# Four expert pairs of a mixture layer sent to their tokens through DRAM instead of by products, in a two-layer decoder trunk on one Trainium2 core

## The chip, the cores and the metric

The kernel runs on one core of a Trainium2 chip. The metric is device time in microseconds (us) of one execution: the median of the kernel before is 1228.84 us over three runs (1222.7 to 1231.54). Engines are named as in the profile: PE (TensorE products), PEld (its weight loads), DVE (VectorE), ACT (ScalarE), POOL (GpSimd), SP (SyncE, which here only issues transfers).

## The reference, cut to what matters

Two layers run on 512 tokens of width 1024. Each has a mixer (attention and gated linear attention) and then a mixture of 32 SwiGLU experts, of which each token uses two. What the change touches is the mixture:

```python
comb = (one_hot(grp_idx, N_GROUPS)[:, :, None] * exp_w[:, None, :])      # two nonzero weights a token
y = zeros_like(hf)
for g in range(N_GROUPS):                                                # 4 groups of 8 experts
    a = einsum('nd,edf->nef', hf, w_gate[g])
    u = einsum('nd,edf->nef', hf, w_up[g])
    y = y + einsum('nef,efd->nd', silu(a) * u * comb[:, g, :, None], w_down[g])
x = x + gate_f * y
```

An expert's weights are three matrices of 1 MB (1024 x 256 in float32): gate, up and down. A layer reads 96 of them.

## The kernel before, in words

The mixture of one layer is `moe`. Tokens are first routed. Each expert has 64 slots, two experts make a pair (128 slots, one per partition), and 16 pairs are worked off in order 0 to 15. I call the position in that order a place. The normalised tokens lie in DRAM (`xg`). For each place:

- `fetch` (POOL, an indirect transfer) brings the rows of the 128 slots, four at first and then two every second place. `gather` turns them with eight PE transposes (tile `g`) and writes them with scale and shift as `gT` (DVE and ACT by turns).
- `hidden`, L1012 on: 16 written products (tile `gu`, 32 instructions in the trace) against gate and up of the two experts; then `silu` on ACT and a product on DVE give `hs`.
- `turn`: two transposes (tile `hsT`) and an ACT copy give `hT`.
- `down`: 8 written products (tile `d`, 16 in the trace) against the down matrices. DVE multiplies by the slots' weights and the gate (L1063, tile `o`); ACT and POOL split that into two float32r halves (L1068 `ohi`, L1069 `olo`).
- `places` builds on DVE a 128x512 matrix with a one where a slot belongs to a token (L1086, L1088), and `combine` multiplies it with the halves: 16 products (tile `y`) for the 8 pieces of 128 tokens x 512 columns, each added to the tokens' rows by DVE (L1076, `add`).

The order on PE is written out. In the loop's step i stand: `down` of place i-1, `hidden` of place i, then the eight `combine` pieces of place i-1 with the transposes of the next gather and `turn` of place i between them. The matmuls made by `pm` keep that order.

The weights come by one queue, SP, in the order of the list `queue`, one 1 MB transfer per matrix. Gate and up share a buffer of 16 KB a partition (`wgu`, five buffers, so two and a half pairs); down has four (`wd`, two pairs). A transfer of `wgu` waits until `hidden` has read the buffer five experts before; one of `wd` until `down` has read the buffer four experts before. SP issues in order: what waits holds up all behind it. The first nine loads are queued ahead of the routing, later ones four at a time after each `hidden`.

```python
queue = [(0, 0), (0, 1), (0, 2), (0, 3), (0, 4), (1, 0), (1, 1), (1, 2), (1, 3)]
for i in range(0, NE, 2):
    queue += [(0, e) for e in (i + 5, i + 6) if e < NE] + [(1, e) for e in (i + 4, i + 5) if e < NE]
```

The tuple's first number is 0 for gate and up, 1 for down; the second is the expert. The last place's products are joined with those of the place before in `combine_last`. Sums and rows of tokens stay in SBUF (`xt`); float32 throughout.

Of the kernel before, what the change touches and what calls it, by code (L numbers as in the profile page):

```python
# [20 lines left out]
P = 128  # L21
# [4 lines left out]
NX = 16  # L26


@with_exitstack
def hybrid_decoder_kernel(ctx, tc, x, c, w_ada, b_ada, norm_mix, norm_ffn, w_in, w_gk2, b_gk, q_gain,  # L30
# [182 lines left out]
    xg = dram.tile([S, D], F, name="xg")  # L213

# [648 lines left out]
    def moe(l, xt, ss, pool):  # L863
# [11 lines left out]
        for i in range(0, NE, 2):  # L875
            queue += [(0, e) for e in (i + 5, i + 6) if e < NE] + [(1, e) for e in (i + 4, i + 5) if e < NE]
# [13 lines left out]
        def load_weights(n):  # L890
            for _ in range(min(n, len(queue))):
                w, e = queue.pop(0)
                loaded[w, e] = load_expert(w, lambda src: src[l, e // 8, e % 8])
# [149 lines left out]
        def down(hT, ws, i=None):  # L1043
# [7 lines left out]
            for q in range(2):  # L1051
# [5 lines left out]
                o = ot([P, 512], name="o")  # L1057
# [4 lines left out]
                else:  # L1062
                    V.scalar_tensor_tensor(o, pd, cws[:, i:i + 1], gate, op0=OP.mult, op1=OP.mult)  # L1063
# [19 lines left out]
        def places(i):  # L1083

            o1 = s2([P, S], name="o1")
            V.tensor_scalar(o1, slots_row[:, 0], sid[:, i:i + 1], None, op0=OP.is_equal)  # L1086
            oT = (rows_ if i == NE // 2 - 1 else ohs)([P, S], R, name="oT")
            V.scalar_tensor_tensor(oT, slots_row[:, 1], sid[:, i:i + 1], o1, op0=OP.is_equal, op1=OP.add)  # L1088
            return oT
# [11 lines left out]
        def combine_last(pairs):  # L1101
# [18 lines left out]
            for n, u in ((0, 5), (0, 6), (1, 0), (1, 1), (0, 7), (1, 2), (1, 3), (1, 4), (1, 5), (1, 6), (1, 7)):  # L1120
                unit(n, u)

# [79 lines left out]
        fetched = [fetch(idx[:, i:i + 1]) for i in range(4)]  # L1202


        with tc.issue_after(listed.ins), tc.issue_after(normed.ins):
# [16 lines left out]
            dump(f"cw{l}", cw)  # L1222
            exw = tmp.rearrange("p t k e -> p (t k) e")
# [22 lines left out]
        hs = None  # L1246
        for i in range(NE // 2):
            while not {(0, 2 * i), (0, 2 * i + 1)} <= set(loaded):
                load_weights(1)
            if i % 2 == 0:  # L1250
                now = gT
                if i < NE // 2 - 2:
                    gT, rest = gather(fetched[i + 2:i + 4])
                    fetched += [fetch(idx[:, j:j + 1]) for j in range(i + 4, min(i + 6, NE // 2))]

            if i:
                part = places(i - 1), down(hT, [loaded.pop((1, e)) for e in (2 * i - 2, 2 * i - 1)], i - 1)
            *_, hs = hidden(gT1 if i == 1 else now, 0 if i < 2 else P * (i % 2), [loaded.pop((0, e)) for e in (2 * i, 2 * i + 1)])
            load_weights(4)
# [5 lines left out]
            if i == 0:  # L1265
                for _ in second:
                    pass
                weights_by_slot()
            for u in range(4):
                for v in range(2):  # L1270
                    if i:
                        combine(2 * u + v, *part)
                next(rest, None)
                if u == 2:
                    hT = turn(hs)
        last = []
# [95 lines left out]
```

## Time and profile before

| what | value |
|---|---|
| median of three runs | 1228.84 us (1222.7 to 1231.54) |
| the profiled execution | 1228.59 us |
| its span, first to last instruction | 1226.4 us |
| mean granted TensorE clock | 0.988 of full |
| PE busy | 1174.6 us, 96% of the span |
| DVE, ACT, POOL busy | 56%, 39%, 16% |
| weights of both mixtures | 2 x 96 transfers of 1 MB, all issued by SP |

Times in the rows are us from the span's start. Layer 1's mixture runs products from about 374 to 625 us, layer 2's from about 968 to the end. "DMA share" in a stretch is the mean busy share of the core's 16 DMA engines, and GB/s what they moved. A releaser in brackets is what ended an idle time. One `issue to landing` is the time of a transfer from its issue to its semaphore.

### The profile page before, as it was taken

To read this page: it belongs to the slowest core of one execution; us is meant where nothing else is said; L and a number is where in the kernel's file an instruction comes from. 1 tells how busy PE (TensorE), PEld (TensorE's weight loads), DVE (VectorE), ACT (ScalarE), POOL (GpSimd) and SP (SyncE) were. 2 spreads that over 40 slices of the span, in tenths; PEclk is the share of its full clock that TensorE was granted. 3 is DMA by queue.
4 is the path that set the end of the run, shared out by engine and by line. 5 is a ranking of instruction groups with operands and counts; after the bars stand their busy time and mean duration, and the time that the engine had idled before them with its cause. 6 is when DMAs were issued, how large, how long until landed. Compare 5 with 4: busy or idle time off the path is not lost.

```text
span 1226.4 us, 17270 instructions
## 1 busy us (share of the span) xinstructions
PE 1174.6 (96%) x6467; PEld 749.3 (61%) x6467; DVE 686.3 (56%) x1336; ACT 473.6 (39%) x942; POOL 196.7 (16%) x231
## 2 busy tenths in 40 slices
PE   4999999999989999999999997999999899999997
PEld 3787867666765444444478775666876744444443
DVE  3474546465854555555566562545856565555553
ACT  4376656453243111111155764554624411111121
POOL 3000010011312222221110001001210222222110
PEclk8999999999999999999999999999999999999999
DMA  9652765643687999999445355563229599999981
GB/s 297 225 170 88 223 167 148 207 142 101 249 369 263 411 410 417 419 418 419 191 156 173 98 168 121 172 172 121 69 103 372 210 400 420 418 420 419 419 349 69
DMA packets 105926, 312.27 MB, mean 255 GB/s; under 512 B 12876, under 2 KB 49936, under 8 KB 81264
## 3 DMA queue, kind: packets, MB, share of 16 engines
q1 hardware_dynamic: 96720, 289.57, 63.4%
q0 software_dynamic: 9120, 21.57, 5.2%
q8 instruction: 52, 0.85, 0.3%
q14 instruction: 34, 0.28, 0.1%
HBM read 311.08 MB, written 8.40 MB: 260 GB/s over the span
## 4 chain that ended last, share of the span: by engine, by line
PE 85%; DMA 6%; DVE 5%; ACT 2%; issue 1%; SPq 1%; DVEq 0%; ACTq 0%
PE proj L74 19%; PE gu L78 18%; PE y L78 10%; PE d L78 9%; PE op L74 6%; PE z L74 5%; DMA wada<-in_w_ada_dram 3%; PE ada L78 3%; PE g L1003 2%; DMA raw<-in_w_in_dram 2%; PE warm L78 1%; PE pv L74 1%; PE lgT L74 1%; PE o L74 1%; PE adaT L78 1%
## 5 line engine op out<-in xcount | busy, mean ns | idle before, releaser
L78 PE MATMUL gu<-wgu,gT 128*64 128x512 f32 x1024 | 225.4, 592 | 0.1
L74 PE MATMUL proj<-whl,hh 128*128 128x512 f32 (+2 forms) x768 | 218.6, 368 | 0.1
L78 PEld LDWEIGHTS gu<-wgu,gT 128*64 128x64 f32 x1024 | 75.5, 137 | 143.7 <-issue 142.2
L74 PEld LDWEIGHTS proj<-whl,hh 128*128 128x128 f32 x768 | 133.5, 189 | 32.0 <-issue 10.0
L1076 DVE TENSOR_TENSOR x<-y,x 128x512 f32<-128x512 f32 x240 | 148.5, 683 | 0.9 <-PE y L78 0.9
L74 PE MATMUL proj<-whl,hl 128*128 128x512 f32 (+2 forms) x384 | 138.4, 362 | 0.0
L1031 DVE TENSOR_TENSOR hs<-hs,gu 128x256 f32<-128x256 f32 x32 | 13.5, 421 | 198.2 <-ACT hs L1030 198.2
L1069 POOL TENSOR_TENSOR olo<-o,ohi 128x512 fp32r<-128x512 f32 x60 | 76.9, 1283 | 263.5 <-ACT ohi L1068 263.3
L96 DVE TENSOR_TENSOR whl<-raw,whl 128x512 fp32r<-128x512 f32 (+2 forms) x128 | 72.7, 570 | 81.8 <-ACT whl L95 70.5
L78 PE MATMUL d<-wd,hT 128*64 128x512 f32 x512 | 116.9, 598 | 1.4 <-ACT hT L1040 1.4
L78 PE MATMUL y<-ohi,oT 128*128 128x512 f32 x240 | 104.5, 436 | 0.0
L95 ACT ACTIVATE whl<-raw 128x512 fp32r<-128x512 f32 (+2 forms) x128 | 66.6, 524 | 85.1 <-PE proj L74 66.9
L78 PE MATMUL y<-olo,oT 128*128 128x512 f32 x240 | 94.2, 393 | 0.0
L74 PEld LDWEIGHTS proj<-whl,hl 128*128 128x128 f32 x384 | 72.2, 188 | 14.3 <-issue 4.2
L1030 ACT ACTIVATE hs<-gu 128x256 f32<-128x256 f32 x32 | 12.3, 385 | 168.4 <-PE gu L78 168.4
L78 PEld LDWEIGHTS d<-wd,hT 128*64 128x64 f32 x512 | 33.9, 136 | 62.2 <-issue 48.1
L78 PEld LDWEIGHTS y<-ohi,oT 128*128 128x128 f32 x240 | 45.4, 189 | 31.8 <-issue 26.0
L1009 ACT ACTIVATE gT<-g,mod 128x256 f32<-128x256 f32 (+1 forms) x72 | 38.9, 544 | 61.6 <-DVE gT L1011 61.5
L1068 ACT ACTIVATE ohi<-o 128x512 fp32r<-128x512 f32 x60 | 37.8, 630 | 61.6 <-DVE o L1063 61.6
L1063 DVE SCALAR_TENSOR_TENSOR o<-d,cws,gate_f 128x512 f32<-128x512 f32 x64 | 47.8, 750 | 22.7 <-PE d L78 22.7
L736 POOL TENSOR_TENSOR raw<-raw,gate_m 128x1024 f32<-128x1024 f32 x16 | 40.2, 2520 | 122.6 <-DMA raw<-in_w_out_dram 68.2
L78 PE MATMUL ada<-wada,ct 128*32 128x512 f32 x320 | 49.1, 600 | 5.3 <-DMA wada<-in_w_ada_dram 5.3
(346 smaller groups left out, 1951.9 us busy)
## 6 DMA issues: line engine op xcount, KB each, us to landing
wgu<-in_w_gate_dram SPq DMA_DIRECT2D x64, 1024.0 KB, 9.5
wgu<-in_w_up_dram SPq DMA_DIRECT2D x64, 1024.0 KB, 11.7
wd<-in_w_down_dram SPq DMA_DIRECT2D x64, 1024.0 KB, 11.0
wada<-in_w_ada_dram SPq DMA_DIRECT2D x96, 512.0 KB, 5.1
raw<-in_w_in_dram SPq DMA_DIRECT2D x80, 256.0 KB, 4.4
raw<-in_w_out_dram SPq DMA_DIRECT2D x16, 512.0 KB, 4.1
raw<-in_w_in_dram SPq DMA_DIRECT2D x32, 128.0 KB, 4.2
xg<-xn POOLq DMA_DIRECT2D x8, 512.0 KB, 4.9
```

The costliest lines, as they stand in the source:

```text
L74: T.matmul(o, a, b, start=start, stop=stop, skip_group_check=True)
L78: tc.keep_in_program_order(T.matmul(o, a, b, start=start, stop=stop, skip_group_check=True))
L95: A.activation(hi, src, AF.Copy)
L96: eng.tensor_tensor(lo, src, hi.bitcast(F), op=OP.subtract)
L736: G.tensor_tensor(t, t, gates[l, 2][:, None, cols].to_broadcast([P, 2, 512]), op=OP.mult)
L1003: tc.keep_in_program_order(T.transpose(ps[:, at:at + P], r[:, P * k:P * k + P], ident))
L1009: A.activation(o, src, AF.Identity, scale=m, bias=b)
L1031: V.tensor_tensor(hs[r], hs[r], gu[r, 256:512], op=OP.mult)
L1063: V.scalar_tensor_tensor(o, pd, cws[:, i:i + 1], gate, op0=OP.mult, op1=OP.mult)
L1068: A.activation(hi, o, AF.Copy)
L1069: (G if last is None else V).tensor_tensor(lo, o, hi.bitcast(F), op=OP.subtract)
L1076: V.tensor_tensor(xc, ps, xc, op=OP.add)
```

## The change

Expert pairs 0 to 3 (the constant `NY`) no longer go to the tokens by products. `ORDER` puts them at places 1, 4, 7 and 10; the other pairs keep the old way. For such a place `down` writes `o` into a slot of the pool that held `ohi` and `olo`, and POOL issues two transfers of 256 KB to a DRAM tile `ys` (128 rows of 4 KB per pair). There is no split, no `places` and no `combine`. Its `down` stands behind the next place's `hidden` instead of before it, so the remaining PE work of that step is four calls of the gather and `turn`.

From place 12 on `take_back` fetches, for each of four token tiles and two choices, the 128 rows that the tokens' slots name (POOL, indirect, rows out of bounds skipped), and DVE adds them times a 0/1 mask to the tokens' rows (128x1024). There are eight of these in a layer: two in each of steps 12 to 14, two behind the loop.

The list of loads follows the order in which buffers come free: before such a place's `down` the gate and up of the next load come first.

```diff
--- before.py
+++ after.py
@@ -24,6 +24,9 @@
 SBW, GKW, GVW, RANK, NIN = 512, 256, 512, 16, 3088
 NE, FE, CAP = 32, 256, 64
 NX = 16
+
+NY = 4
+ORDER = [4, 0, 5, 6, 1, 7, 8, 2, 9, 10, 3, 11, 12, 13, 14, 15]
 
 
 @with_exitstack
@@ -211,6 +214,7 @@
 
     xs = dram.tile([S, D], F, name="xs")
     xg = dram.tile([S, D], F, name="xg")
+    ys = dram.tile([NY * P, D], F, name="ys")
 
     mod = [const.tile([P, 6, KT], F, name=f"mod{l}") for l in range(L)]
     gates, gms, rowt = {}, {}, {}
@@ -872,8 +876,12 @@
         s1 = slots(pool, "s1", 4, 1024)
 
         queue = [(0, 0), (0, 1), (0, 2), (0, 3), (0, 4), (1, 0), (1, 1), (1, 2), (1, 3)]
-        for i in range(0, NE, 2):
-            queue += [(0, e) for e in (i + 5, i + 6) if e < NE] + [(1, e) for e in (i + 4, i + 5) if e < NE]
+
+        freed = [(0, 0)]
+        for i in range(1, NE // 2):
+            freed += [(0, i), (1, i - 1)] if ORDER[i - 1] < NY else [(1, i - 1), (0, i)]
+        for w, i in freed:
+            queue += [(w, e) for e in ((2 * i + 4, 2 * i + 5) if w else (2 * i + 5, 2 * i + 6)) if e < NE]
         loaded = {}
 
         def load_expert(which, src):
@@ -890,7 +898,8 @@
         def load_weights(n):
             for _ in range(min(n, len(queue))):
                 w, e = queue.pop(0)
-                loaded[w, e] = load_expert(w, lambda src: src[l, e // 8, e % 8])
+                n = 2 * ORDER[e // 2] + e % 2
+                loaded[w, e] = load_expert(w, lambda src: src[l, n // 8, n % 8])
 
         load_weights(9)
         wr, lc, lg = route.pop(l)
@@ -1054,13 +1063,17 @@
                     for e in range(n):
                         pm(pd[64 * e:64 * e + 64], hT[:, j, 64 * e:64 * e + 64],
                            ws[e][:, D * j + 512 * q:D * j + 512 * q + 512], j == 0, j == 1)
-                o = ot([P, 512], name="o")
+                m = NY if i is None else ORDER[i]
+                o = (ohl if m < NY else ot)([P, 512], name="o")
                 gate = gates[l, 5][r, 512 * q:512 * q + 512]
                 if i is None:
                     V.tensor_tensor(o[r], pd[r], gate, op=OP.mult)
                     parts.append(o)
                 else:
-                    V.scalar_tensor_tensor(o, pd, cws[:, i:i + 1], gate, op0=OP.mult, op1=OP.mult)
+                    V.scalar_tensor_tensor(o, pd, cws[:, m:m + 1], gate, op0=OP.mult, op1=OP.mult)
+                    if m < NY:
+                        kept_dma(G, ys[P * m:P * m + P, 512 * q:512 * q + 512], o)
+                        continue
                     if last is not None:
                         hi, lo = last[:, q, 0], last[:, q, 1]
                     else:
@@ -1083,9 +1096,10 @@
         def places(i):
 
             o1 = s2([P, S], name="o1")
-            V.tensor_scalar(o1, slots_row[:, 0], sid[:, i:i + 1], None, op0=OP.is_equal)
+            n = ORDER[i]
+            V.tensor_scalar(o1, slots_row[:, 0], sid[:, n:n + 1], None, op0=OP.is_equal)
             oT = (rows_ if i == NE // 2 - 1 else ohs)([P, S], R, name="oT")
-            V.scalar_tensor_tensor(oT, slots_row[:, 1], sid[:, i:i + 1], o1, op0=OP.is_equal, op1=OP.add)
+            V.scalar_tensor_tensor(oT, slots_row[:, 1], sid[:, n:n + 1], o1, op0=OP.is_equal, op1=OP.add)
             return oT
 
         units = [(tt, q) for tt in range(NT) for q in range(2)]
@@ -1119,6 +1133,16 @@
             yield
             for n, u in ((0, 5), (0, 6), (1, 0), (1, 1), (0, 7), (1, 2), (1, 3), (1, 4), (1, 5), (1, 6), (1, 7)):
                 unit(n, u)
+
+        ysi, ysm = pool.tile([P, NT, 2], I32, name="ysi"), t3(2, "ysm")
+
+        def take_back(tt, k):
+
+            r = rows_([P, D], name="back")
+            G.indirect_dma_start(r, None, ys[:, :], bass.IndirectOffsetOnAxis(ap=ysi[:, tt, k:k + 1], axis=0),
+                                 bounds_check=NY * P - 1, oob_is_err=False)
+            xc = xt[tt // 2][:, tt % 2]
+            return lambda: V.scalar_tensor_tensor(xc, r, ysm[:, tt, k:k + 1], xc, op0=OP.mult, op1=OP.add)
 
         def spread(slot, slot0):
 
@@ -1199,7 +1223,7 @@
         idx = pool.tile([P, NE // 2], I32, name="idx")
         listed = numbered(by_slot(exn, "nv"), idx)
         keep_warm(lo.rearrange("p t e -> p (t e)"), 20)
-        fetched = [fetch(idx[:, i:i + 1]) for i in range(4)]
+        fetched = [fetch(idx[:, i:i + 1]) for i in ORDER[:4]]
 
 
         with tc.issue_after(listed.ins), tc.issue_after(normed.ins):
@@ -1220,6 +1244,8 @@
             V.tensor_tensor(e2, e2, den, op=OP.mult)
             V.tensor_tensor(cw[:, :, 1:2], e2, gw, op=OP.mult)
             dump(f"cw{l}", cw)
+            V.tensor_scalar(ysi, slot, 65535.0, None, op0=OP.min)
+            V.tensor_scalar(ysm, slot, float(NY * P), None, op0=OP.is_lt)
             exw = tmp.rearrange("p t k e -> p (t k) e")
             V.tensor_tensor(exw, ex.rearrange("p t k e -> p (t k) e"), cw.rearrange("p t k -> p (t k)")[:, :, None].to_broadcast([P, NT * 2, NE]), op=OP.mult)
         cws = pool.tile([P, NE // 2], F, name="cws")
@@ -1243,7 +1269,7 @@
         for _ in rest:
             pass
         gT1, second = gather(fetched[1:2])
-        hs = None
+        back, taken = [(tt, k) for tt in range(NT) for k in range(2)], []
         for i in range(NE // 2):
             while not {(0, 2 * i), (0, 2 * i + 1)} <= set(loaded):
                 load_weights(1)
@@ -1251,11 +1277,14 @@
                 now = gT
                 if i < NE // 2 - 2:
                     gT, rest = gather(fetched[i + 2:i + 4])
-                    fetched += [fetch(idx[:, j:j + 1]) for j in range(i + 4, min(i + 6, NE // 2))]
-
-            if i:
+                    fetched += [fetch(idx[:, j:j + 1]) for j in ORDER[i + 4:i + 6]]
+
+            by_dram = i > 0 and ORDER[i - 1] < NY
+            if i and not by_dram:
                 part = places(i - 1), down(hT, [loaded.pop((1, e)) for e in (2 * i - 2, 2 * i - 1)], i - 1)
             *_, hs = hidden(gT1 if i == 1 else now, 0 if i < 2 else P * (i % 2), [loaded.pop((0, e)) for e in (2 * i, 2 * i + 1)])
+            if by_dram:
+                down(hT, [loaded.pop((1, e)) for e in (2 * i - 2, 2 * i - 1)], i - 1)
             load_weights(4)
             if i == 1:
                 overflow_lists()
@@ -1266,13 +1295,26 @@
                 for _ in second:
                     pass
                 weights_by_slot()
+            if by_dram:
+                for _ in range(4):
+                    next(rest, None)
+                hT = turn(hs)
+                continue
             for u in range(4):
                 for v in range(2):
                     if i:
                         combine(2 * u + v, *part)
+                if i >= NE // 2 - 4 and u % 2 == 0:
+                    taken.append(take_back(*back.pop(0)))
+                    if len(taken) > 1:
+                        taken.pop(0)()
                 next(rest, None)
                 if u == 2:
                     hT = turn(hs)
+        for tt, k in back:
+            taken.append(take_back(tt, k))
+        for add_back in taken:
+            add_back()
         last = []
         end = combine_last([part, last])
         next(end)
```

First, PE at places 9 to 11. Before, the steps of two places meet like this (`g` are the transposes of a gather, `hsT` those of `turn`):

```order
L1003 MATMUL g<-ident,rows 128x128 x2
L1038 MATMUL hsT<-ident,hs 128x128 x2
L78 MATMUL y<-ohi,oT 128x512
L78 MATMUL y<-olo,oT 128x512
L78 MATMUL y<-ohi,oT 128x512
L78 MATMUL y<-olo,oT 128x512
L1003 MATMUL g<-ident,rows 128x128 x2
L78 MATMUL d<-wd,hT 64x512 x8
L78 MATMUL gu<-wgu,gT 64x512 x16
L78 MATMUL y<-ohi,oT 128x512
L78 MATMUL y<-olo,oT 128x512
```

Now, where place 10 (expert pair 3) ends, the rows from the last two products of place 9 on are these:

```order
L81 MATMUL y<-ohi,oT 128x512
L81 MATMUL y<-olo,oT 128x512
L1012 MATMUL g<-ident,rows 128x128 x2
L81 MATMUL gu<-wgu,gT 64x512 x16
L81 MATMUL d<-wd,hT 64x512 x8
L1012 MATMUL g<-ident,rows 128x128 x8
L1047 MATMUL hsT<-ident,hs 128x128 x2
L81 MATMUL d<-wd,hT 64x512 x8
L81 MATMUL gu<-wgu,gT 64x512 x16
L81 MATMUL y<-ohi,oT 128x512
L81 MATMUL y<-olo,oT 128x512
```

The `d` of place 10 has moved behind the `gu` of place 11, the `d` of place 11 follows after ten transposes only, and no `y` of place 10 stands between them.

Second, SP's loads from expert 25 on. The numbers are the buffers' tiles; before, `wgu_4849` to `wgu_4960` are gate and up of experts 25 to 28 in places 12 to 14, and `wd_4855`, `wd_4857` are the down matrices of place 12:

```order
L887 DMA wgu_4849<-in_w_gate_dram 128x2048
L887 DMA wgu_4849<-in_w_up_dram 128x2048
L887 DMA wgu_4852<-in_w_gate_dram 128x2048
L887 DMA wgu_4852<-in_w_up_dram 128x2048
L883 DMA wd_4855<-in_w_down_dram 128x2048
L883 DMA wd_4857<-in_w_down_dram 128x2048
L887 DMA wgu_4957<-in_w_gate_dram 128x2048
L887 DMA wgu_4957<-in_w_up_dram 128x2048
L887 DMA wgu_4960<-in_w_gate_dram 128x2048
L887 DMA wgu_4960<-in_w_up_dram 128x2048
```

Now gate and up of places 12 to 14 are `wgu_4728` to `wgu_4737`, the down matrices of place 12 are `wd_4828` and `wd_4830`, those of place 13 `wd_4832` and `wd_4834`:

```order
L895 DMA wgu_4728<-in_w_gate_dram 128x2048
L895 DMA wgu_4728<-in_w_up_dram 128x2048
L895 DMA wgu_4731<-in_w_gate_dram 128x2048
L895 DMA wgu_4731<-in_w_up_dram 128x2048
L895 DMA wgu_4734<-in_w_gate_dram 128x2048
L895 DMA wgu_4734<-in_w_up_dram 128x2048
L895 DMA wgu_4737<-in_w_gate_dram 128x2048
L895 DMA wgu_4737<-in_w_up_dram 128x2048
L891 DMA wd_4828<-in_w_down_dram 128x2048
L891 DMA wd_4830<-in_w_down_dram 128x2048
L891 DMA wd_4832<-in_w_down_dram 128x2048
L891 DMA wd_4834<-in_w_down_dram 128x2048
```

The down matrices of place 12 stood ahead of the gate and up of experts 27 and 28, and now stand behind them: four more 1 MB transfers are ahead of them. The same holds at places 3, 6 and 9.

Third, POOL at the end of a mixture. Before, the last fetches and the halves:

```order
L983 DMA rows<-xg,idx 128x1024 x2
L1069 TENSOR_TENSOR olo<-o,ohi 128x512 x4
L983 DMA rows<-xg,idx 128x1024 x2
L1069 TENSOR_TENSOR olo<-o,ohi 128x512 x4
L983 DMA rows<-xg,idx 128x1024 x2
L1069 TENSOR_TENSOR olo<-o,ohi 128x512 x12
L1281 TENSOR_LOAD xcnt
```

Now, from the last fetches on (`ys` are the writes to DRAM, `back` the rows that come back):

```order
L91 DMA ys<-o 128x512 x2
L1082 TENSOR_TENSOR olo<-o,ohi 128x512 x2
L992 DMA rows<-xg,idx 128x1024 x2
L1082 TENSOR_TENSOR olo<-o,ohi 128x512 x2
L91 DMA ys<-o 128x512 x2
L1142 DMA back<-ys,ysi 128x1024
L1082 TENSOR_TENSOR olo<-o,ohi 128x512
L1142 DMA back<-ys,ysi 128x1024
L1082 TENSOR_TENSOR olo<-o,ohi 128x512
L1142 DMA back<-ys,ysi 128x1024
L1082 TENSOR_TENSOR olo<-o,ohi 128x512 x2
L1142 DMA back<-ys,ysi 128x1024 x4
```

The first `back` stands between the last two `ys` writes and the halves of place 11, and the others among the halves of places 11 to 13.

## Rows read from the trace of the kernel before

**Rows 1.** The page: busy time of PE over the span, then the granted clock, the DMA engines' busy share and their GB/s in 40 equal slices of 30.7 us.

```profile
PE 1174.6 (96%) x6467; PEld 749.3 (61%) x6467; DVE 686.3 (56%) x1336; ACT 473.6 (39%) x942; POOL 196.7 (16%) x231
...
DMA  9652765643687999999445355563229599999981
GB/s 297 225 170 88 223 167 148 207 142 101 249 369 263 411 410 417 419 418 419 191 156 173 98 168 121 172 172 121 69 103 372 210 400 420 418 420 419 419 349 69
```

**Rows 2.** Windows of layer 1's mixture: us, busy time of each engine (and its instructions), granted clock, DMA share, GB/s. The first lies ahead of the first product of an expert, when nine loads were queued at once; the last lies behind the mixture and holds a write to DRAM.

```profile
330.00:345.00 15.00, 15.00 (x72) 12.20 (x71) 11.58 (x19) 7.70 (x18) 0.00 (x0) 1.00 1.01 422
390.00:450.00 60.00, 60.00 (x290) 28.72 (x288) 35.53 (x67) 11.64 (x23) 14.15 (x12) 1.00 1.00 410
450.00:510.00 60.00, 60.00 (x289) 28.50 (x286) 32.57 (x58) 11.79 (x24) 14.22 (x12) 1.00 1.01 418
510.00:560.00 50.00, 50.00 (x241) 23.34 (x241) 29.36 (x53) 10.14 (x20) 9.65 (x8) 1.00 1.01 419
...
630.00:645.00 15.00, 14.14 (x86) 12.13 (x87) 11.46 (x22) 9.89 (x16) 3.13 (x5) 1.00 0.99 346
```

**Rows 3.** What SP's queue waited for, 390 to 560 us: waiter, releaser, us in total, times, longest.

```profile
SPq L883 <- PE d L78: 72.6, 11, 7.1
SPq L887 <- PE gu L78: 64.7, 11, 6.0
```

**Rows 4.** PE's timeline at one place of layer 1: start, us, line and operation, count.

```profile
551.98 0.50 PE L78 MATMUL y<-ohi,oT 128*128 128x512 f32 x1
...
556.99 3.65 PE L78 MATMUL d<-wd,hT 128*64 128x512 f32 x16
560.48 2.74 PE L78 MATMUL gu<-wgu,gT 128*64 128x512 f32 x12
```

**Rows 5.** PE's timeline elsewhere: eight transposes of a gather by themselves, and a `turn` with its `d` right behind it, with the wait between.

```profile
373.21 1.09 PE L1003 MATMUL g<-ident,rows 128*128 128x128 f32 x8 [0.19 <-DMA rows<-xg,idx]
...
615.35 0.39 PE L1038 MATMUL hsT<-ident,hs 128*128 128x128 f32 x2
616.20 3.65 PE L78 MATMUL d<-wd,hT 128*64 128x512 f32 x16 [0.46 <-ACT hT L1040]
```

**Rows 6.** The second down matrix of place 12 in layer 1: its issue on SP, then its transfer (KB, us from issue to landing), then the products that read it.

```profile
545.63 0.38 SPq L883 DMA_DIRECT2D wd<-in_w_down_dram  x1
...
wd<-in_w_down_dram SPq DMA_DIRECT2D x1, 1024.0 KB, 12.9
...
572.45 3.65 PE L78 MATMUL d<-wd,hT 128*64 128x512 f32 x16
```

**Rows 7.** The same three for layer 2.

```profile
1139.36 1.02 SPq L883 DMA_DIRECT2D wd<-in_w_down_dram  x1
...
wd<-in_w_down_dram SPq DMA_DIRECT2D x1, 1024.0 KB, 13.5
...
1166.18 3.65 PE L78 MATMUL d<-wd,hT 128*64 128x512 f32 x16
```

**Rows 8.** Layer 1's last gate and up load (expert 31): the issue of its up matrix, that transfer, and the first products of place 15, which read it.

```profile
583.38 0.42 SPq L887 DMA_DIRECT2D wgu<-in_w_up_dram  x1
...
wgu<-in_w_up_dram SPq DMA_DIRECT2D x1, 1024.0 KB, 10.4
...
605.97 1.46 PE L78 MATMUL gu<-wgu,gT 128*64 128x512 f32 x6
```

**Rows 9.** The page's groups of instructions: busy us, mean ns of one, idle time before them and its releaser.

```profile
L1076 DVE TENSOR_TENSOR x<-y,x 128x512 f32<-128x512 f32 x240 | 148.5, 683 | 0.9 <-PE y L78 0.9
L1069 POOL TENSOR_TENSOR olo<-o,ohi 128x512 fp32r<-128x512 f32 x60 | 76.9, 1283 | 263.5 <-ACT ohi L1068 263.3
L1063 DVE SCALAR_TENSOR_TENSOR o<-d,cws,gate_f 128x512 f32<-128x512 f32 x64 | 47.8, 750 | 22.7 <-PE d L78 22.7
```

**Rows 10.** Transfers issued by POOL: count, KB each, median us from issue to landing.

```profile
xg<-xn POOLq DMA_DIRECT2D x8, 512.0 KB, 4.9
xs<-x POOLq DMA_DIRECT2D x2, 1024.0 KB, 10.7
rows<-xg,idx POOLq DMA_INDIRECT x32, 8.6
```

**Rows 11.** The granted clock around three idle times of PE in layer 2 (columns as in rows 2).

```profile
757.50:762.80 5.30, 1.42 (x11) 0.91 (x10) 0.00 (x0) 0.00 (x0) 1.50 (x3) 1.00 0.61 58
762.80:769.60 6.80, 4.35 (x12) 3.23 (x12) 4.43 (x7) 4.62 (x9) 2.13 (x4) 0.50 0.48 122
889.00:892.40 3.40, 1.30 (x10) 0.49 (x8) 3.29 (x6) 0.54 (x1) 1.08 (x1) 1.00 0.19 26
892.50:895.90 3.40, 3.40 (x18) 2.29 (x15) 1.43 (x4) 0.60 (x1) 1.29 (x1) 0.50 0.34 127
957.40:960.80 3.40, 3.40 (x26) 3.17 (x25) 2.73 (x10) 0.00 (x0) 0.00 (x0) 0.50 0.39 161
```

**Rows 12.** Those idle times, in PE's timeline, and one that no fall of the clock followed (at 630.76).

```profile
765.25 1.11 PE L500 MATMUL qT<-ident,two 128*128 128x128 f32 x4 [6.33 <-ACT w L553]
...
891.29 2.08 PE L74 MATMUL pv<-w,v 128*64 128x512 f32 x8 [2.10 <-DVE mixl L96]
...
957.32 0.18 PE L78 MATMUL rk<-both,after_b 128*128 128x32 bf16 x1 [2.16 <-DVE both L951]
...
630.76 1.49 PE L78 MATMUL warm<-ident 128*128 128x128 f32 x11 [2.04 <-DVE sm L100]
```

## The prediction

> **What bounds the kernel now.** I read the page's slices first. PE is busy for 96% of the span, and in the slices of the two mixtures the DMA engines show a 9 as well, at 410 to 420 GB/s [rows 1]. So in just the stage that is changed two resources look full, and the question is which of them has room.
>
> The windows of layer 1's mixture say it more sharply. From 390 to 560 us PE is busy 60.00 of 60, 60.00 of 60 and 50.00 of 50 us: it waits for no weight at all. The DMA share is 1.00 to 1.01, at 410 to 419 GB/s. When nine loads had been queued at once, ahead of the first expert product, with none waiting for a buffer, the rate was 422 GB/s [rows 2]. So 420 is what this core's DMA moves when it is never short of requests, and the mixture runs at it. SP does wait for PE to release buffers, 72.6 us for `d` and 64.7 us for `gu` [rows 3], but not long enough for the engines to run dry. Each is just fast enough for the other: PE sets the end, and the transfers follow a little ahead of it.
>
> How far ahead is the number that decides. The second down matrix of place 12 was issued at 545.63 and landed 12.9 us later, at 558.5; its products began at 572.45: 13.9 us to spare [rows 6]. In layer 2 it landed at 1139.36 + 13.5 = 1152.9 and was read from 1166.18: 13.3 us to spare [rows 7]. The last gate and up load landed at 583.38 + 10.4 = 593.8, and place 15 began at 605.97: 12.2 us [rows 8].
>
> **The change part by part.** *PE.* One place's `y` stretch, with its transposes among the products, runs from 551.98 to 556.99, 5.0 us [rows 4]. In its stead stand eight transposes (1.1 us), a `turn` of 0.4 us and a wait of 0.5 us for ACT's copy, since no product is left to cover it [rows 5]: 2.0 us. Four places save 4 x 3.0 = 12.0 us of PE in a layer, 24 in both.
>
> *The other engines.* DVE loses 32 additions of 683 ns a layer (21.9 us) and gains eight of 128x1024. No row has that operation. The nearest is a scalar-tensor-tensor of half the columns at 750 ns [rows 9]; from once to twice that, and I take twice, 1.5 us, 12 us in all. DVE is busy 29 of 50 us [rows 2], so this costs nothing while the fetched rows are there in time. POOL loses eight halves of 1.28 us. Issuing a `back` waits for the last `ys` write, and behind it in POOL's queue stand the halves of place 11, which `y` of place 11 reads. A gap opens there only if a write takes longer than place 11's `d` and place 12's `gu` together (3.5 us from 556.99 to 560.48 [rows 4], and 7.0 us, which is what is left of the 15.46 us from one `d` to the next [rows 4, 6] without 3.5 and 5.0), plus the transposes; the writes of `xg` landed in 4.9 us and the fetches in 8.6 [rows 10]. And what PE loses there it loses ahead of a longer wait, below. Nothing.
>
> *The transfers.* Here the change only adds. Each layer writes 8 x 256 KB. At 420 GB/s a write takes 0.62 us of all 16 engines; in the window that holds the write of `xs` the engines were as full (0.99) and moved only 346 GB/s [rows 2], which makes 0.76. I take 0.69, 5.5 us a layer. The ends are 0 (if POOL's transfers found idle gaps; a share of 1.00 leaves none) and 2.45 us (half of the 4.9 us in which 512 KB of `xg` landed [rows 10]). The rows that come back, a quarter of 1024 rows of 4 KB, are 1 MB or 2.5 us, but are fetched from place 12 on.
>
> The Trainium skill's page "DMA: Bandwidth & Descriptors" says, in "Issuing engines are not separate DMA queues", that transfers started by different engines end up on the same 16 DMA engines and interleave. By that rule the writes, though POOL's, take their full time out of the weights' stream, all eight even where some are issued late; the full DMA share agrees, and without the rule the low end of 0 would stand beside 5.5.
>
> *The order of the loads.* `down` of places 1, 4, 7 and 10 now stands behind the next `gu`, so its buffers come free 3.5 us after those of that `gu` instead of 7 us before, and SP issues the latter's four transfers first. Nothing issued behind them lands earlier on that queue: the spacing is one 1 MB after the other, 1,048,576 B at 420 GB/s or 2.5 us. For the down matrices of place 12 that is 4 x 2.5 = 10.0 us more ahead of them. At the same time PE wants them sooner, since `d` of places 10 and 11 stand together.
>
> *Sum.* Since the DMA engines never pause, a faster PE doesn't make them earlier. The second down matrix of place 12 lands 10.0 + 5.5 = 15.5 us later than before, with 13.9 us to spare in layer 1 and 13.3 in layer 2: `d` of place 12 starts 1.6 and 2.2 us later than it did. The 12 us that PE saves turn into waits for down matrices at places 6, 9 and 12, the last of 4 to 7 us. From there to the end of the layer the products are those of before (five places by the old way, no write among them), the loads still to come land ahead of PE, and nothing is won back: 3.8 us for both layers.
>
> *The clock.* Waits of PE have a price of their own. After idle times of 2.10, 2.16 and 6.33 us the granted clock stood at 0.50 (1.2 of 2.4 GHz), with 3.4 us of products at that rate in two cases and 4.35 in the third; after one of 2.04 us it stayed at 1.00 [rows 2, 11, 12]. Half of that is lost, 1.7 to 2.2 us; I take 1.9. At places 6 and 9 the next wait swallows it; at place 12 nothing does: 2 x 1.9 = 3.8 us.
>
> The Trainium skill's page "TensorE: Matmul & The Clock Gate", in "HAM oscillation — how this bites in real kernels", describes products throttled again after each wait for a transfer. The rows agree that a wait can be followed by half rate; without that rule the sum would be 3.8 us lower.
>
> The profiled execution took 1228.59 us, within 0.3 us of the median of 1228.84. 1228.59 + 3.8 + 3.8 = 1236.2.
>
> **The rivals.**
>
> *PE's saving is kept whole.* If the DMA engines had room, both layers would end 12 us earlier: 1228.59 - 24 = 1204.6. For it speaks that PE is at 100% and SP's waits are for PE; against it, that the share is 1.00 and the rate within 3% of the one with nothing to wait for.
>
> *The order of loads doesn't bind.* If the down matrices of place 12 were served beside the four transfers and not behind them, the next limit would be the load for place 15. It would land at 593.8 + 5.5 + 1.9 (six of eight `back`s) = 601.2, and place 15 start 4.8 us earlier than 605.97: 9.6 in both, 1219.0. Against it: transfers of SP land one after the other.
>
> *The writes are dear* (the other side). The place is the same down matrix of place 12; the price is the time in which a 256 KB write keeps the engines from weights. Each 0.1 us over 0.69 costs 0.8 us a layer. At 1.3 us, between my value and the far end of 2.45, it is 8 x 0.61 x 2 = 9.8 us more: 1246. From about 1.0 us a write on, the change is slower by over 1%. For it: 346 GB/s with a write in the window; against it: that window's loads were also of small pieces.
>
> **How the numbers follow.** A difference of about 1%, 12.3 us, is what a measurement of this kernel can tell from no change; that is 1216.5 and 1241. I give the forecast 0.60, the first rival 0.08, the second 0.14, the third 0.18. The forecast's own range: low, if writes take 0.62 (1.2 us less in both layers), the clock doesn't fall (3.8 less) and the DMA engines make up the 2 to 3 us a layer by which 410 to 419 GB/s fell short of 422 (5 less), 1226; high, with 0.76 (1.2 more), the dearer fall (0.6) and a `back` that holds up DVE for 1.5 us a layer, 1241. To hold 8 in 10 it reaches to the second rival and into the third: 1217 to 1244. Faster takes the first rival and a part of the second, 0.12; slower most of the third and the forecast's edge, 0.16; within 1% the rest, 0.72.
>
> **What would show it.** In the profile after: PE waiting for `wd` transfers at places 6, 9 and 12 of each layer, some 10 us a layer in all, where none stood; DMA share still 1.0 over the mixture; the second down matrix of place 12 landing at about 574 us, with `d` right behind it and a granted clock of 0.5 in the next 3 to 4 us; PE's busy time some 20 us lower; the same stretch from there to the end of the layer. It is wrong if PE shows no such waits, if the loads end with the engines idle between them, or if DVE or POOL waits hold up `y`.

## The result, and the profile after

| | before | after |
|---|---|---|
| median | 1229.99 us (4 runs) | 1242.3 us (4 runs, 1236.94 to 1243.18) |
| ratio | | 1.012, interval 1.0087 to 1.0152 |
| profiled execution, its span | 1228.59, 1226.4 us | 1242.67, 1240.9 us |
| first product of `gu` at place 0 to the end of `d` at place 15, layer 1 and 2 | 245.48, 245.49 us | 249.28, 251.16 us |

The ratio stands with its 95% interval; the two medians alone give 1.010. The change is slower by 1.2%; the forecast was 0.6%. The page after, beside [rows 1]: PE's busy time, the DMA engines' share and GB/s in 40 slices (of 31.0 us), and the queue of POOL's transfers (packets, MB, share of 16 engines).

```profile
PE 1161.8 (94%) x6339; PEld 730.4 (59%) x6339; DVE 664.5 (54%) x1276; ACT 462.4 (37%) x926; POOL 206.7 (17%) x247
...
DMA  9753765643687999999554354563229599999981
GB/s 298 228 159 98 209 166 158 192 157 99 255 341 299 408 418 420 420 419 419 220 187 154 87 174 104 170 187 120 58 105 418 221 386 420 421 420 420 418 360 69
...
q0 software_dynamic: 12704, 28.19, 6.6%
```

PE is busy 12.8 us less, in a span 14.5 us longer. The slices of the mixtures move the same GB/s as before. The windows of layer 1 (columns as in [rows 2]) put the two together:

```profile
390.00:450.00 60.00, 59.48 (x288) 26.90 (x286) 31.64 (x61) 10.84 (x22) 12.85 (x12) 1.00 1.01 407
450.00:510.00 60.00, 55.03 (x256) 23.42 (x254) 23.18 (x40) 9.46 (x20) 11.57 (x12) 0.97 1.01 419
510.00:560.00 50.00, 47.72 (x226) 20.62 (x224) 21.88 (x37) 8.80 (x18) 8.36 (x8) 1.00 1.02 421
```

PE, at 60, 60 and 50 before, now waits in each window, and the DMA engines are as full as they were. PE does save what was forecast where nothing holds it up: from `d` of place 0 to `d` of place 2 the kernel before took 30.92 us,

```profile
386.93 3.65 PE L78 MATMUL d<-wd,hT 128*64 128x512 f32 x16 [0.24 <-ACT hT L1040]
417.85 3.65 PE L78 MATMUL d<-wd,hT 128*64 128x512 f32 x16
```

and the changed one 27.79, which is 3.1 us less a moved place and 12.5 a layer:

```profile
387.89 3.65 PE L81 MATMUL d<-wd,hT 128*64 128x512 f32 x16 [0.24 <-ACT hT L1049]
415.68 3.65 PE L81 MATMUL d<-wd,hT 128*64 128x512 f32 x16 [0.52 <-ACT hT L1049]
```

What PE waits for in layer 1 from 380 us on, and in layer 2 from 975 us on (waiter, releaser, us in total, times, longest):

```profile
PE d L81 <- DMA wd<-in_w_down_dram: 8.3, 6, 2.6
PE d L81 <- ACT hT L1049: 2.8, 6, 0.5
PE y L81 <- POOL olo L1082: 1.6, 1, 1.6
...
PE d L81 <- DMA wd<-in_w_down_dram: 6.9, 4, 3.6
```

No wait for `wd` stood there before. PE's timeline at place 6 and place 12 of layer 1, then at place 12 of layer 2 (beside [rows 6, 7]; a bracket holds the idle time and what ended it):

```profile
477.09 1.04 PE L81 MATMUL d<-wd,hT 128*64 128x512 f32 x2 [2.58 <-DMA wd<-in_w_down_dram]
479.49 4.83 PE L81 MATMUL d<-wd,hT 128*64 128x512 f32 x13 [1.36 <-DMA wd<-in_w_down_dram]
...
573.76 1.04 PE L81 MATMUL d<-wd,hT 128*64 128x512 f32 x2 [1.27 <-DMA wd<-in_w_down_dram]
576.15 3.22 PE L81 MATMUL d<-wd,hT 128*64 128x512 f32 x13 [1.34 <-DMA wd<-in_w_down_dram]
...
1174.35 1.04 PE L81 MATMUL d<-wd,hT 128*64 128x512 f32 x2
1176.91 3.22 PE L81 MATMUL d<-wd,hT 128*64 128x512 f32 x13 [1.52 <-DMA wd<-in_w_down_dram]
```

Each `d` begins on its first matrix, does two products and waits again for the second. The second waits end at 576.15 and 1176.91 us, which tells when the second down matrix of place 12 landed (this trace holds no landing of its own for it). Counted from the layer's first `gu` (374.98 and 973.85) that is 201.2 and 203.1 us; before it was 184.1 and 184.8 (558.5 and 1152.9 of [rows 6, 7], less 374.38 and 968.11). It lands 17.0 and 18.3 us later; the forecast was 15.5. The granted clock around these waits (columns as in [rows 2]):

```profile
473.00:479.40 6.40, 2.56 (x12) 1.23 (x10) 4.22 (x8) 1.41 (x3) 0.00 (x0) 1.00 1.01 422
479.40:482.80 3.40, 3.31 (x8) 1.00 (x10) 0.00 (x0) 0.00 (x0) 0.00 (x0) 0.50 1.01 419
570.00:573.70 3.70, 2.49 (x14) 1.82 (x12) 3.70 (x6) 0.84 (x2) 0.02 (x1) 1.00 1.02 412
573.80:577.20 3.40, 2.06 (x8) 0.61 (x10) 2.40 (x5) 0.56 (x1) 0.89 (x1) 1.00 1.01 417
577.20:580.60 3.40, 3.40 (x20) 1.12 (x17) 1.45 (x2) 0.63 (x1) 0.91 (x1) 1.00 1.02 413
```

At place 6 it falls to 0.50; at place 12, behind two waits of 1.27 and 1.34 us with products between them, it stays at 1.00. The other engines and transfers, beside [rows 9, 10]:

```profile
L1089 DVE TENSOR_TENSOR x<-y,x 128x512 f32<-128x512 f32 x176 | 109.7, 680 | 3.0 <-PE y L81 3.0
...
ys<-o POOLq DMA_DIRECT2D x16, 256.0 KB, 7.2
rows<-xg,idx POOLq DMA_INDIRECT x32, 8.5
back<-ys,ysi POOLq DMA_INDIRECT x16, 8.5
```

Where the 14.1 us between the two profiled executions lie:

| stretch | after less before | forecast |
|---|---|---|
| start to layer 1's first `gu` | +0.6 | 0 |
| first `gu` to the end of `d` at place 12, both layers | +3.1, +5.0 | +1.6, +2.2, and 1.9 each for the clock |
| from there to the end of `d` at place 15 | +0.7, +0.7 | 0 |
| between the mixtures | +1.3 | 0 |
| end of the last `d` to the end of the span | +3.0 | 0 |
| around the span | -0.4 | 0 |

The 1.3 us between the mixtures are no more than kernels differ there anyway: in the first four runs below, and before and after, this stretch took 345.1 to 349.7 us.

### The profile page after: what moved, and what is told of

Same layout as the page of the kernel before. It is cut to its first block, busy times and chain, and to the rows that moved or that the text cites. A ratio compares the mean times of both kernels' runs of the same rounds, so it can differ in the third digit from the quotient of the medians.

```text
span 1240.9 us, 17036 instructions
## 1 busy us (share of the span) xinstructions
PE 1161.8 (94%) x6339; PEld 730.4 (59%) x6339; DVE 664.5 (54%) x1276; ACT 462.4 (37%) x926; POOL 206.7 (17%) x247
## 3 DMA queue, kind: packets, MB, share of 16 engines
q0 software_dynamic: 12704, 28.19, 6.6%
## 5 line engine op out<-in xcount | busy, mean ns | idle before, releaser
L81 PE MATMUL gu<-wgu,gT 128*64 128x512 f32 x1024 | 231.4, 593 | 0.1
L81 PE MATMUL d<-wd,hT 128*64 128x512 f32 x512 | 128.9, 619 | 22.4 <-DMA wd<-in_w_down_dram 15.2
L1089 DVE TENSOR_TENSOR x<-y,x 128x512 f32<-128x512 f32 x176 | 109.7, 680 | 3.0 <-PE y L81 3.0
L81 PEld LDWEIGHTS d<-wd,hT 128*64 128x64 f32 x512 | 37.5, 142 | 96.5 <-issue 68.1
L1082 POOL TENSOR_TENSOR olo<-o,ohi 128x512 fp32r<-128x512 f32 x44 | 59.6, 1360 | 131.4 <-ACT ohi L1081 119.6
L81 PE MATMUL y<-ohi,oT 128*128 128x512 f32 x176 | 77.0, 438 | 0.3 <-DVE x L1089 0.3
L81 PE MATMUL y<-olo,oT 128*128 128x512 f32 x176 | 69.7, 396 | 2.3 <-POOL olo L1082 2.3
L1081 ACT ACTIVATE ohi<-o 128x512 fp32r<-128x512 f32 x44 | 27.7, 630 | 86.6 <-DVE o L1073 82.2
L1049 ACT COPY hT<-hsT 128x256 f32<-128x256 f32 x32 | 11.9, 373 | 111.4 <-PE hsT L1047 111.4
## 6 DMA issues: line engine op xcount, KB each, us to landing
wgu<-in_w_gate_dram SPq DMA_DIRECT2D x64, 1024.0 KB, 13.7
wd<-in_w_down_dram SPq DMA_DIRECT2D x64, 1024.0 KB, 15.5
```

What stands on the lines that cost most here:

```text
L81: tc.keep_in_program_order(T.matmul(o, a, b, start=start, stop=stop, skip_group_check=True))
L1081: A.activation(hi, o, AF.Copy)
L1082: (G if last is None else V).tensor_tensor(lo, o, hi.bitcast(F), op=OP.subtract)
L1089: V.tensor_tensor(xc, ps, xc, op=OP.add)
```

## The experiments

The first four ran beside a kernel before of 1225.48 us (31 runs), the last four beside one of 1226.44 (15 runs); ratios are to these, with a 95% interval, and need not be the quotient of two medians. "Mixture" is the stretch of the first table. My theory was that the transfers are full, and that the order of loads and the late `down` pin place 12; the main rival, that the writes are dear.

**e1_oldqueue.** The changed kernel with the list of loads of before.

```diff
-        freed = [(0, 0)]
-        ...
+        for i in range(0, NE, 2):
+            queue += [(0, e) for e in (i + 5, i + 6) if e < NE] + [(1, e) for e in (i + 4, i + 5) if e < NE]
```

> The change, with the loads in the order of before (down matrices of a place ahead of the next gate and up). Theory A (the order of the loads pins the down matrices of place 12, and the DMA engines have no room): the waits for down matrices at places 6, 9 and 12 go, since 10 us of loads no longer stand ahead of them; but SP now stands 3.5 us at each moved down, so gate and up come late instead and PE waits for them around places 8 to 11 and 13. About 2 us a layer under the change: 1237 to 1240. Rival B (the writes to DRAM are what costs): no wait changes, 1242. Rival C (the moved transposes and turns on PE cost it): 1242.

1231.42 us, ratio 1.0056 (1.0025 to 1.0086); mixtures 246.35 and 245.3. PE's waits in layer 1:

```profile
PE gu L81 <- DMA wgu<-in_w_up_dram: 5.4, 3, 3.1
...
PE y L81 <- POOL olo L1079: 1.7, 1, 1.7
```

About half of the loss goes, more than I had expected. The waits for down matrices are gone, and waits for gate and up stand in their place: with `down` late, SP's queue stands behind it, and for once the DMA engines are not full (0.96 and 387 GB/s, beside 1.00 and 410 in [rows 2]):

```profile
390.00:450.00 60.00, 59.48 (x288) 26.90 (x286) 32.00 (x65) 11.16 (x23) 13.41 (x12) 1.00 0.96 387
```

**e2_early.** The same, and `down` of the four places back in front of `hidden`.

```diff
-            if i and not by_dram:
+            if by_dram:
+                down(hT, [loaded.pop((1, e)) for e in (2 * i - 2, 2 * i - 1)], i - 1)
+            elif i:
                 part = ...
             *_, hs = hidden(...)
-            if by_dram:
-                down(hT, [loaded.pop((1, e)) for e in (2 * i - 2, 2 * i - 1)], i - 1)
```

> The change with the order of loads of before, and the down of places 1, 4, 7 and 10 back in front of the next place's hidden, so that their buffers come free as early as the others. Theory A: no wait for a down matrix; PE keeps its saving until the lead of the transfers (13 us) is used up, then waits 3 to 4 us a layer for gate and up from place 13 on. 4 to 5 us a layer under the kernel before, less 2 to 3 us of a longer end: 1222 to 1226. Rival B (writes): the waits stay, 1238 to 1242. Rival C (PE's rearranged steps): this edit makes them worse, a wait for ACT's copy right behind the turn, 1242 or more.

1220.03 us, ratio 0.9962 (0.9939 to 0.9985); mixtures 241.78 and 241.92. Four pairs through DRAM, with all their writes, are faster than before once neither `down` nor its loads come late. Two waits for gate and up are left in a layer, 3.4 us in layer 1:

```profile
PE gu L81 <- DMA wgu<-in_w_up_dram: 3.4, 2, 2.0
...
PE d L81 <- DMA wd<-in_w_down_dram: 1.0, 1, 1.0
```

**e3_nowrites.** The changed kernel without the writes and the rows back; it leaves out the four pairs' results.

```diff
-                        kept_dma(G, ys[P * m:P * m + P, 512 * q:512 * q + 512], o)
                         continue
...
-                    taken.append(take_back(*back.pop(0)))
```

> The change without its writes to DRAM and without the rows that come back: the four pairs' results are left out of the sums. Theory A: only the writes' share of the delay goes, 8 x 0.8 to 0.95 us a layer; the waits for down matrices at place 12 stay, shorter by 2 to 3 us; 5 to 6 us a layer less, and 2 us less at the end: 1228 to 1231, about the kernel before. Rival B (the writes are what costs): the waits go altogether and PE's saving of 12 us a layer shows: 1206. Rival C: 1240.

1221.53 us, ratio 0.998 (0.9955 to 1.0006); mixtures 241.28 and 243.71. The second down matrix of place 12 landed 193.8 and 196.3 us after the first `gu`, 9.7 and 11.5 later than before: that is the part of the loads' order with the late `down`, which e3 keeps, and 7.3 and 6.8 are left for the writes and rows back. The time is some 7 us under what the theory had: beside the changed kernel the mixtures fell by 8.0 and 7.5 us, where I expected 5 to 6, and the kernel before beside it is 4.5 us faster than the one I had started from. PE still waits, in layer 1:

```profile
PE d L81 <- DMA wd<-in_w_down_dram: 4.3, 4, 1.4
```

Behind place 12 the stretch took 43.8 us, as before: the 0.7 us a layer belong to the rows back.

**e4_before_writes.** The kernel before with eight unread 256 KB writes a layer.

```diff
+                    if i in (1, 4, 7, 10):
+                        m = i // 3
+                        kept_dma(G, ys[P * m:P * m + P, 512 * q:512 * q + 512], o)
```

> The kernel before, with the same 8 writes of 256 KB a layer added (places 1, 4, 7 and 10, the product of down with the slots' weights), and nothing else. They are not read. Theory A: each write keeps the DMA engines 0.8 to 0.95 us, so the second down matrix of place 12 lands 6 to 8 us later, still 6 us ahead of its products; no wait on PE: 1229 to 1233, with 1 to 2 us of that at the very end, where POOL's drain took longer in the changed kernel. Rival B (dear writes): over 1.7 us a write, then PE waits at place 12 and the time is 1236 or more.

1225.63 us, ratio 1.0015 (0.9993 to 1.0037); mixtures 245.49 and 245.50, unchanged. The same matrix landed 4.6 and 5.5 us later than before, 0.58 and 0.69 us a write, and found its time to spare:

```profile
450.00:510.00 60.00, 60.00 (x290) 28.72 (x288) 32.46 (x58) 11.62 (x23) 16.56 (x16) 1.00 1.01 419
510.00:560.00 50.00, 50.00 (x242) 23.14 (x240) 28.93 (x51) 10.34 (x20) 11.51 (x11) 1.00 1.02 421
```

PE is full again. The writes take their full time out of SP's stream and cost nothing while 13.9 us are to spare. The Trainium skill's page "DMA: Bandwidth & Descriptors" ("Issuing engines are not separate DMA queues") has it that transfers of different engines interleave on the same 16; these 4.6 and 5.5 us agree.

**e5_early_nowrites.** e2 without writes and rows back (the results of the four pairs are left out): e2's and e3's edits together.

> The changed kernel with the loads in the order of before, `down` of the four places back in front of `hidden`, and neither the writes to `ys` nor the rows back (it leaves out the four pairs' results): what PE's saving is worth with nothing else added. Theory (the added transfers take their time out of the weights' stream): the waits of 3.8 to 4.4 us a layer that stood with the writes go, both mixtures fall from 241.8/241.9 to 237 to 239 us, and the whole is 1209 to 1215 against a before of 1226. Rival (four places save PE less than I worked out, some 2 us each instead of 3): mixtures 240.5 to 242, the whole 1217 to 1220, and no waits for weights either way.

1206.16 us, ratio 0.984 (0.9801 to 0.9878); mixtures 235.16 and 236.10. It is faster than either had it: the mixtures are 10.3 and 9.4 us shorter than before. From `d` of place 1 to `d` of place 2 it takes 12.52 us, where 15.46 were (556.99 to 572.45 in [rows 4, 6]), so PE saves 2.9 a place, 11.8 a layer:

```profile
402.96 3.65 PE L81 MATMUL d<-wd,hT 128*64 128x512 f32 x16
415.48 3.65 PE L81 MATMUL d<-wd,hT 128*64 128x512 f32 x16 [0.52 <-ACT hT L1046]
```

It doesn't keep quite all of it: `gu` of place 12 takes 7.8 and 8.8 us instead of 7.0, in layer 2 with a wait for an up matrix in it:

```profile
1131.93 1.51 PE L81 MATMUL gu<-wgu,gT 128*64 128x512 f32 x6 [0.72 <-DMA wgu<-in_w_up_dram]
```

Layer 1's windows:

```profile
450.00:510.00 60.00, 58.96 (x286) 25.07 (x284) 23.57 (x41) 10.70 (x22) 11.66 (x10) 1.00 1.01 419
510.00:560.00 50.00, 49.48 (x234) 23.03 (x231) 22.25 (x40) 8.16 (x17) 7.09 (x6) 1.00 1.02 420
```

The DMA moves no more than before; what is spent is the lead. The second down matrix of place 12 landed 185.5 us after the first `gu` and was read at 187.7: of 13.9 us to spare 2.2 are left. With the writes and rows back, in e2, the mixtures are 6.6 and 5.8 us longer than here: what cost nothing in e4 is paid once the lead is gone.

**e6_three_early.** e2 with three pairs, at places 1, 4 and 7.

```diff
-NY = 4
-ORDER = [4, 0, 5, 6, 1, 7, 8, 2, 9, 10, 3, 11, 12, 13, 14, 15]
+NY = 3
+ORDER = [3, 0, 4, 5, 1, 6, 7, 2, 8, 9, 10, 11, 12, 13, 14, 15]
```

> Three pairs through DRAM (at places 1, 4 and 7) instead of four, `down` in front of `hidden`, the loads in the order of before: the best version by the theory, since two writes a layer fewer leave the last gate and up loads ahead of PE again. Theory: waits for weights under 1 us a layer, mixtures 241 to 243 us, the whole 1217 to 1222 against a before of 1226 (ratio 0.993 to 0.997), about equal to four pairs. Rival (each place saves in proportion, and the waits cost nothing): a quarter of the gain is lost, ratio 0.997 to 0.998.

1217.81 us, ratio 0.9929 (0.9902 to 0.9955), faster than both kernels; mixtures 240.75 and 240.57. Waits for weights fell to 0.5 and 1.3 us a layer, where the theory had less than 1. The rival, that a quarter of the gain is lost, falls; that three pairs are better than four is not shown, since the two intervals overlap. Layer 1:

```profile
PE gu L81 <- DMA wgu<-in_w_up_dram: 0.5, 2, 0.3
```

**e7_small_writes.** The kernel before with 32 unread writes of one row of 2 KB, for the drain with which POOL's program ends.

```diff
+                        for v in range(2):
+                            kept_dma(G, ys[2 * m + v:2 * m + v + 1, 512 * q:512 * q + 512], o[v:v + 1])
```

> The kernel before with 32 tiny unread writes by POOL (one row of 2 KB each; 16 a layer). POOL's last instruction, a drain, took 1.94 us before, 3.16 us with 16 writes of 128 rows, 3.98 us with the change's 32 transfers. If it goes by the count of POOL's transfers, it takes 4 us here; if by their rows (descriptors), 1.9 to 2.0. The time itself: 1226 to 1229.

1226.78 us (one run). The drain took 3.57 us: nearer to 4 than to 2, so the number of POOL's transfers sets it more than their size.

**e8_writes_twice.** The changed kernel with each write made twice.

```diff
+                        kept_dma(G, yt[P * m:P * m + P, 512 * q:512 * q + 512], o)
                         kept_dma(G, ys[P * m:P * m + P, 512 * q:512 * q + 512], o)
```

> The changed kernel with each write to `ys` made twice (the second to a DRAM tile that nobody reads): what a write costs where PE already waits for the weights. Theory, with the writes taking their share of full DMA engines: at 0.58 to 0.68 us each (as eight unread writes showed in the kernel before), the second down matrix of place 12 lands 4.6 to 5.5 us later after the mixture's start than 201.2/203.05, the mixtures become 254 and 256 us, the whole 1251 to 1254 against a before of 1230. Rival (a write costs more here, 0.85 to 0.91, which is the difference between the changed kernel with and without its writes): 6.8 to 7.3 us later, the whole 1256 to 1258.

1251.86 us, ratio 1.0206 (1.0165 to 1.0247); mixtures 257.23 and 256.91. The first down matrix of place 12 in layer 1 landed 5.1 us later than in the changed kernel, the second in layer 2 3.8 later: 0.64 and 0.47 us a write, so the rival's price falls. But the mixtures are longer than the theory had them, for another reason, and that the whole came out in its range is luck: it was worked out from a kernel before of 1230, and the one beside it took 1226.44. Layer 1's waits:

```profile
PE y L81 <- POOL olo L1084: 7.5, 4, 3.4
PE d L81 <- DMA wd<-in_w_down_dram: 5.8, 3, 3.1
```

`take_back` on POOL waits for the last writes, the halves stand behind it, and `y` of place 11 waits for them, with the clock at half rate behind that wait (second row, columns as in [rows 2]):

```profile
568.90 1.06 POOL L1144 DMA_INDIRECT back<-ys,ysi  x1 [11.54 <-DMA ys<-o]
...
572.50:579.40 6.90, 5.59 (x18) 4.43 (x18) 3.75 (x7) 0.00 (x0) 1.25 (x1) 0.51 1.03 417
```

`d` of place 12 no longer waits for its matrix there; it comes 10.3 and 8.3 us later than in the changed kernel (counted from the first `gu`) because PE does.

## Why the prediction was right or wrong

*The mechanism held.* PE's saving turned into waits for down matrices at places 6, 9 and 12, the DMA stayed full, and place 12 was pinned by a matrix that came 17 to 18 us later against 13 to 14 to spare. e1 and e2 show the causes one at a time: the loads' order by release costs 0.6% (1.012 to 1.0056), the late `down` another 0.9% (1.0056 to 0.9962). The writes and rows back cost 1.4% (1.012 to 0.998, e3). Such shares need not add up, since all three draw on the same lead.

*What failed is the sum.* It had 3.8 us for late transfers, and 8.1 were measured; it had 3.8 for the clock at place 12, and nothing came; and it had nothing for the stretch behind place 12 and for the end of the program, where 1.4 and 3.0 us stood. That the whole was off by no more than 6.5 us (14.1 against 7.6, between the profiled executions) is in part luck: the clock's 3.8, which did not come, stood in for a part of the 10 us that were missing.

*The transfers' term was too small.* The sum had 10.0 + 5.5 = 15.5 us; measured were 17.0 and 18.3. The order's 10.0 was 9.7 and 11.5 in e3. For the writes the 0.69 us each is about what was measured (0.58 and 0.69 in e4, 0.64 and 0.47 in e8). But the step "are fetched from place 12 on" failed: the first two `back`s were issued at 563.14 and 565.68, ahead of the landing at 576.15, and a third at 573.68. The rows back moved 28.19 - 21.57 - 4.19 (16 writes) = 2.4 MB in 16 transfers, at 420 GB/s 0.36 us each if they are alike, so two add 0.7 by this estimate. Writes and two `back`s make 5.3 to 6.2 of the 7.3 and 6.8 us; the remaining 0.6 to 2.0 stay unexplained. Since the lead was spent already, each of these us went straight into the time: 8.1 instead of 3.8. I had counted the spare to the start of `d`, whose first products read the first matrix; the second is wanted some 0.5 us later, which is small beside the rest.

*The clock's term did not come.* I took 1.9 us a layer behind one wait of 4 to 7 us at place 12. The wait there was cut in two by the two matrices, and smaller (2.6 us together; 1.5 in layer 2), since PE had lost most of its saving by then. Before, `d` of place 11 began 182.6 us after the first `gu` (556.99 of [rows 4] less 374.38). With 12.5 us saved it would have begun at 170.1; it began at 180.0 and 183.8 (555.02 and 1157.69), so 9.9 and 13.7 us were lost ahead of it, at places 6 and 9 above all. There the clock did fall (at 479.4 us in layer 1, 1076.7 and 1127.9 in layer 2), and as forecast the next wait swallowed it: PE still waited for its matrix at place 12. The falls also account for most of why PE's busy time is 12.8 us lower and not the forecast's 20: the clock stood at 0.50 for 13.6 us of the two mixtures, in which products are busy some 6 us longer than at full rate, by this estimate. The Trainium skill's page "TensorE: Matmul & The Clock Gate" ("HAM oscillation — how this bites in real kernels") tells of half rate after each wait for a transfer; here that held at place 6 of both layers and place 9 of layer 2, but neither at place 9 of layer 1 (waits of 0.42 and 1.35 us) nor at place 12.

*Behind place 12, and the end of the program.* I had written "nothing is won back" and counted nothing as lost. The rows back cost 0.7 us a layer there (e3), and the program's end 3.0 us. Of these the drain took 2.0 (3.98 against 1.94). The other 1.0 also stands in e3 and e5, which have neither writes nor rows back (13.9 us from the end of the last `d` to the end of the span, 12.9 before), so it is not a price of the added transfers, and its cause stays open. The sum had no line for what comes after the last product.

*`take_back` at nothing.* It was 1.6 and 0.7 us of PE's time, ahead of the wait for the matrix, so nothing in this kernel; e8 shows that it is next in line. The condition that I gave for it was wrong, though. The gap was to open only if a write took longer than `d` and `gu` together, 10.5 us; the last write took 7.9 (554.37 to 562.31), and the gap opened. I had left out POOL's own time behind the write, two issues of a `back` and two halves:

```profile
563.14 1.06 POOL L1142 DMA_INDIRECT back<-ys,ysi  x1 [8.19 <-DMA ys<-o]
564.23 1.28 POOL L1082 TENSOR_TENSOR olo<-o,ohi 128x512 fp32r<-128x512 f32 x1
565.68 1.03 POOL L1142 DMA_INDIRECT back<-ys,ysi  x1 [0.17 <-PE gu L81]
566.73 1.28 POOL L1082 TENSOR_TENSOR olo<-o,ohi 128x512 fp32r<-128x512 f32 x1
...
568.06 0.50 PE L81 MATMUL y<-olo,oT 128*128 128x512 f32 x1 [1.62 <-POOL olo L1082]
```

The addition of the rows back on DVE took 1.27 us, where I took 1.5.

*The rivals.* "The writes are dear" falls with e4 and e8. "The order of loads doesn't bind" falls with e1. "PE's saving is kept whole" is what e5 shows, but for 0.8 and 1.8 us, with the transfers and the order taken away. So the time came out near the dear writes' (1246) for another reason: a write cost about what I took, and what was missing were the rows back, the order's larger share in layer 2, a part that stays unexplained, and the end of the program.

## What to carry to other kernels

Where two resources run level, the lead of one over the other is a sum that can be spent once: add up all that draws on it before calling any part free. Here the later landing of 17 us and PE's own saving of some 12 drew on 13.9; the 15 us too many ate the saving and 3 us more. When work is moved to a later point, move it last on paper too: the transfers that wait for its buffers, and all that is queued behind them, move with it. Where the work stands can weigh more than how much of it is moved: four pairs with a late `down` lost 1.2%, the same four with `down` and the loads in their old places gained 0.4%, and three gained 0.7% (the last two can't be told apart).

## What the runs showed of the hardware

The drain at the end of POOL's program grew with the transfers that POOL had issued: 1.94 us before, 3.16 with 16 more, 3.73 with 28, 3.98 with 32, 5.37 with 48, and 3.57 with 32 tiny ones.

Waits of one size went with either level of the clock. At place 12 of layer 1, after 1.27 and 1.34 us with two products between, it stayed at 1.00. At place 9 of layer 2, PE's timeline and the windows of the clock (columns as in [rows 2]) show it fall behind waits of 1.23 and 1.35 us:

```profile
1126.18 1.04 PE L81 MATMUL d<-wd,hT 128*64 128x512 f32 x2 [1.23 <-DVE x L1089]
1128.57 4.56 PE L81 MATMUL d<-wd,hT 128*64 128x512 f32 x13 [1.35 <-DMA wd<-in_w_down_dram]
```

```profile
1124.50:1127.90 3.40, 1.50 (x6) 0.33 (x3) 3.20 (x6) 0.79 (x2) 2.08 (x2) 1.00 1.01 419
1127.90:1131.30 3.40, 2.73 (x8) 0.88 (x10) 0.00 (x0) 0.00 (x0) 0.00 (x0) 0.50 1.02 424
```

So the length of a wait alone, from which I had worked, doesn't tell whether the clock falls.
